# Seven products for eight in an up projection: Strassen's scheme for the ConvFFN of a one-core decoder step

## The chip, the core and the metric

The kernel runs on one core of one Trainium2 chip. TensorE (PE in the profile, with its weight loads as PEld) multiplies; VectorE (DVE), ScalarE (ACT) and GpSimd (POOL) do the elementwise work; SyncE (SP) issues most transfers. Each engine has a queue of its own and takes its instructions in order; semaphores tie the queues together. A matmul writes to PSUM, from which DVE and ACT read; the other operands lie in SBUF.

The metric is the device time of one execution in microseconds.

## The reference

One inference step of a decoder layer, for 512 prompt positions and a sample group of 8 sequences with 4 positions each, together 544 tokens of width 1024. The mixer (input projection, RG-LRU branch, sliding-window attention, gates, output projection, norms) comes first and is all but untouched by the change. What matters is the feed-forward part behind it:

```python
def _conv_ffn(h, prev, w_up, conv_w, conv_b, w_down):
    u = h @ w_up                                             # 1024 -> 8192
    u, conv_state = _causal_dwconv(u, prev, conv_w, conv_b)  # width 3, over positions
    val, gate = jnp.split(u, 2, axis=-1)
    return (jax.nn.gelu(gate, approximate=True) * val) @ w_down, conv_state   # 4096 -> 1024
...
    f, ffn_state = _conv_ffn(_rmsnorm(x, norm_ffn_pre[l]), ffn_prev, w_up[l], ffn_conv_w[l], ffn_conv_b[l], w_down[l])
    x = x + _rmsnorm(f, norm_ffn_post[l])
```

All inputs and outputs are float32. Outputs are y for both groups and the new states, among them the last two rows of u before the convolution.

## The kernel before

**Precision.** A product in float32 is made of three matmuls in a reduced format: each operand is split into a high and a low part, and high x high, high x low and low x high are summed in PSUM. A weight tile is loaded in float32 ("raw", 512 KB), and split in two units of 128x512: ACT writes the high part (`wsplit_hi`, L271), DVE subtracts it from the raw tile for the low part (`wsplit_lo`, L276). Activations are split in the same way.

**Tiling.** Everything is feature-major: 128 features on the partitions, 544 tokens along them. Tokens are taken in two halves of 256 and 288 (`HALF`). One half column tile of a projection is 8 k x 3 = 24 matmuls into one PSUM bank (`mmhalf`, all matmuls at L144), followed by its evacuation (`done`) and a round of side work (`tick`, `sides`).

**Feed-forward.** The 8192 columns of w_up are 64 column tiles: tile p (value) and tile 32 + p (gate) form a pair. Four pairs' first token halves are computed early, while the second half of the tokens is still in its norms (`norm_chain`). `up_a` and `up_b` copy the halves into a tile `u` (ACT, L1121 and L1129; the sample columns by DVE, L1130), move the convolution states (POOL, L1128, L1131, L1132), and convolve in three taps: the first on ACT (L1134), two on DVE (the helper `stt`, L156). `glu` applies GELU (ACT, L1142) and multiplies (DVE, `z`), then splits the result into `fH` and `fL` (ACT L1149; the helper `sub`, L147). The down projection runs in four quarters of the 4096 features: 8 pairs, then 8 column tiles x 2 halves of 24 matmuls each, `pmdn`. Quarter 0 is copied out of PSUM by ACT (L1225), later ones are added to `ft` by DVE (the helper `add`, L153). The last quarter takes the second token half first; its final norm (`finish_b`: statistics `pst_o`, `rep_o`, POOL additions at L1254, transposes `pyo` at L1262) runs under the products of the first half, whose own end is `finish_a` (L1274).

**Order.** PE's order is the program's order throughout. ACT's and DVE's are so in the mixer and left to a planner in the feed-forward part; POOL's and SP's are the planner's. Tiles come from rings of buffers (53 slots "s", 10 temporaries, 5 raw weight tiles, 12 split units, 8 PSUM banks): a step whose ring is full waits for the oldest user to finish. Splits run a fixed number of column tiles ahead of their use (`upto`).

Of the kernel before, what the change touches and what calls it, by code (L numbers as in the profile page):

```python
# [17 lines left out]
P = 128  # L18
# [7 lines left out]
HALF = ((0, 256), (256, NT))  # L26
NH = 8
# [12 lines left out]
S_BUFS = 53  # L40
# [3 lines left out]
SLOT = 576  # L44
LEAD = 2
NORM_TICKS = (2.5, 3.5)
HP = 150
NSTART = (1, 1)
YA = (1, 1)
YB = (1, 1)  # L50
EARLY = 8
# [52 lines left out]
def hawk_step(ctx, tc, I, O):  # L104
# [3 lines left out]
    cp = ctx.enter_context(tc.tile_pool(name="const", bufs=1))  # L108
# [10 lines left out]
    mixer = ExitStack()  # L119
    mixer.enter_context(tc.manual_schedule(engines={act.engine, dve.engine}))  # L120
# [37 lines left out]
    # Side work runs in stages between the half column tiles of the main products. A half tile's results are  # L158
    # taken out of PSUM while the next one runs.
# [32 lines left out]
    ident = cp.tile([P, P], F32, name="ident")  # L192
    make_identity(nc, ident)
    ones = cp.tile([P, P], F32, name="ones")
    pool.memset(ones, 1.0)
    epst = cp.tile([P, 1], F32, name="epst")
    pool.memset(epst, EPS)

# [1 line left out]
    w_in, w_up, w_dn = I["w_in"][0], I["w_up"][0], I["w_down"][0]  # L200

    def wsrc(key):
        kind = key[0]
        if kind in ("wr", "wi"):
            return I["lru_" + kind][0, 4 * key[1]:4 * key[1] + 4].rearrange("n c d -> c n d")
        w = {"in": w_in, "lo": I["w_lru_o"][0], "ao": I["w_attn_o"][0], "out": I["w_out"][0], "up": w_up,
             "dn": w_dn}[kind]
        c = key[-1]
        if kind == "dn":
            w = w[key[1] * D:(key[1] + 1) * D, :]  # L210
        return w[:, c * P:(c + 1) * P].rearrange("(k p) n -> p k n", p=P)
# [9 lines left out]
    ffn_seq = []  # L221
    nxt = 0
    for q in range(4):
        while nxt < min(32, 8 * q + 8 + LEAD):
            ffn_seq.append(("pair", nxt))
            order += [("up", nxt), ("up", 32 + nxt)]
            nxt += 1
        ffn_seq.append(("down", q))
        order += [("dn", q, c) for c in range(8)]
    early_up = [("up", j) for p_ in range(EARLY // 2) for j in (p_, 32 + p_)]  # L230
    wpos = {k: i for i, k in enumerate(order)}
    in_slots = {("out", c) for c in range(3, 8)} | {("dn", 3, c) for c in range(3, 7)} | set(early_up[3:])
    in_slots |= {("in", c) for c in qkv_order[3:FIRST]}
    in_temps = {("dn", 3, 7)}
# [15 lines left out]
    def wclaim(target):  # L250
        """Units (half column tiles) up to the target that are not split yet; loads run two tiles ahead."""
        target = min(target, 2 * len(order))
        for i in range(len(wraw), min(len(order), (target + 1) // 2 + 2)):
            if target:
                wload(i)
        got = list(range(wnext[0], target))
        wnext[0] = max(wnext[0], target)
        return got

    def wsplit_hi(un):  # L260
        i, u = un // 2, un % 2
        hl = []
        for x in "hl":
            if order[i] in in_slots or order[i] in in_temps:
                t_ = (S if order[i] in in_slots else T)(f"w{x}{u}_{wname(i)}", F32R)[:, 0:512]
# [15 lines left out]
    class Full:  # L281
        """Eight operand tiles [P, NT], high and low parts."""

        def __init__(self, name):
            self.name, self.t = name, {}
# [5 lines left out]
        def get(self, k, a, j):  # L291
            lo, hi = HALF[a]
            return self.t[k][j][:, lo:hi]

    class Halves:
        """Eight operand tiles, two to a slot, the token halves apart."""
# [4 lines left out]
        def get(self, k, a, j):  # L301
            n = HALF[a][1] - HALF[a][0]
            if (k // 2, a) not in self.t:
                self.t[k // 2, a] = [S(f"{self.name}{x}{k // 2}_{a}", F32R) for x in "HL"]
            return self.t[k // 2, a][j][:, (k % 2) * n:(k % 2 + 1) * n]

    def mmhalf(ps, key, X, a, ks=range(KD)):
        n = HALF[a][1] - HALF[a][0]
        if key == order[0] and a == 0:
            # the parts in the order in which they get ready  # L310
# [34 lines left out]
    warm = cp.tile([P, 1], F32, name="warm")  # L345
# [26 lines left out]
    pv = cp.tile([P, 96], F32, name="pv")  # L372
    # keeps the tensor engine's clock up until the first tokens are there
# [7 lines left out]
    def newton_rstd(r, v, s_, sq):  # L381
        """r = (sq / D + EPS) ** -0.5 from the hardware's square root and one Newton step."""
# [80 lines left out]
    fv = cp.tile([P, 256], F32, name="fv")  # L463
# [10 lines left out]
    # recurrent states: rows 0..23 conv (b, i), rows 24..31 h0 (b)  # L474
# [7 lines left out]
    def params():  # L482
# [13 lines left out]
        # c = 8 softplus(-lambda) = 8 (max(-lambda, 0) + log1p(exp(-|lambda|)))  # L496
# [39 lines left out]
    def attn_tables():  # L536
# [6 lines left out]
        # one copy of each head's row per query, read back with a row pitch one short: the Toeplitz band  # L543
# [32 lines left out]
    # shifted part of the sample caches goes straight through DRAM  # L576
# [70 lines left out]
    def softmax_a(s3, nh, sink, nm):  # L647
        """s3 [P, nh, n] scores to exponentials in place; sink [P, nh]."""
# [150 lines left out]
    stage = cp.tile([P, KD, 36], F32, name="stage")  # L799
    L = Full("l")  # L800
# [130 lines left out]
    # the first column tiles run on the first token half alone while the second is still being normed  # L931
# [23 lines left out]
    # while softmaxes run, the gates' logits wait for their sigmoids  # L955
# [24 lines left out]
    # x again, feature-major, for the residual  # L980
# [19 lines left out]
    M = Halves("m")  # L1000

    def lo_done(c):
        def f(a, ps):
            lo, hi = HALF[a]
# [16 lines left out]
    def stats(acc, nch, nm, more=None):  # L1021
        """acc [P, 128 nch]: squares summed over feature tiles; returns rstd [P (tokens), nch]."""
# [17 lines left out]
    def spread(dg, n, nm):  # L1040
        """The diagonal of rstd (tokens) to a row replicated over the partitions, in PSUM."""
# [14 lines left out]
    h2 = Halves("h2_")  # L1056
    mt = [S(f"mt{c}") for c in range(8)]

    def norm_chain(a, acc):
        lo, hi = HALF[a]  # L1060
        n = hi - lo
        nch = (n + P - 1) // P
        with tc.high_priority(offset=HP):
            dg = diag(stats(acc, nch, f"m{a}"), n, f"m{a}")
        yield YA[a]
        with tc.high_priority(offset=HP):
            rep = spread(dg, n, f"m{a}")
            acc2 = T(f"accx{a}")
            for c in range(8):
                m_ = mt[c][:, lo:hi]  # L1070
                stt(m_, m_, pv[:, G_POST + c:G_POST + c + 1], rep[:, :n], ALU.mult, ALU.mult)
                pool.tensor_tensor(out=x1[c][:, lo:hi], in0=x1[c][:, lo:hi], in1=m_, op=ALU.add)  # L1072
                sq_sum(acc2, x1[c][:, lo:hi], n, c == 0, f"x{a}_{c}")
        yield NORM_TICKS[a]
        with tc.high_priority(offset=HP):
            dg = diag(stats(acc2, nch, f"f{a}"), n, f"f{a}")
        yield YB[a]
        with tc.high_priority(offset=HP):
            rep = spread(dg, n, f"f{a}")
            for c in range(8):  # L1080
                t_ = T(f"h2t{a}_{c}")
                stt(t_[:, :n], x1[c][:, lo:hi], pv[:, G_FPRE + c:G_FPRE + c + 1], rep[:, :n], ALU.mult, ALU.mult)
                act.activation(h2.get(c, a, 0), t_[:, :n], AF.Copy)
                sub(h2.get(c, a, 1), t_[:, :n], f32(h2.get(c, a, 0)))

    def out_done(c, acc):
        def f(a, ps):
            lo, hi = HALF[a]
# [4 lines left out]

    for a in range(2):
        acc = T(f"acc{a}")
        for c in range(8):
            target = upto(("out", c), 1, 3) if a == 0 else 2 * (wpos["up", 0] + min(c, EARLY))
            step(("out", c), M, a, out_done(c, acc), target=target, quick=True)
        start_at(now[0] + NSTART[a], norm_chain(a, acc))

# [1 line left out]
    # conv states: DRAM rows (b, i) of 8192 seen as (b, i, m) rows of 1024  # L1102
    sfT = cp.tile([P, KD, 16, 8], F32, name="sfT")
    stage_p = cp.tile([P, KD, 2, 8], F32, name="stage_p")
    sf_rows = RAW("sf_rows")
    nc.sync.dma_start(out=sf_rows, in_=I["state_ffn_conv"].rearrange("o b i (m n) -> (o b i m) n", n=D))
    ut = {}
# [10 lines left out]
    def up_a(j, ps):  # L1118
        u = ut[j] = T(f"u{j}")
        pool.memset(u[:, 0:2], 0.0)  # L1120
        act.activation(u[:, 2:258], ps[:, 0:256], AF.Copy)  # L1121

    def up_b(j, ps):
        m, c = j // 8, j % 8
        u = ut[j]
        uv = u[:, SEQ + 2:SEQ + 2 + 6 * DB].rearrange("p (b i) -> p b i", b=DB)
        sv = sfT[:, c, :, m].rearrange("p (b i) -> p b i", b=DB)
        pool.tensor_copy(uv[:, :, 0:2], sv)  # L1128
        act.activation(u[:, 258:514], ps[:, 0:256], AF.Copy)  # L1129
        dve.tensor_copy(uv[:, :, 2:6], ps[:, 256:288].rearrange("p (b t) -> p b t", b=DB))  # L1130
        pool.tensor_copy(sv, uv[:, :, 4:6])  # L1131
        pool.tensor_copy(stage_p[:, c, :, m], u[:, SEQ:SEQ + 2])  # L1132
        y = T(f"uc{j}")
        act.activation(y[:, 0:FLATU], u[:, 0:FLATU], AF.Copy, scale=fv[:, j:j + 1])  # L1134
        for t in (1, 2):
            stt(y[:, 0:FLATU], u[:, t:t + FLATU], fv[:, 64 * t + j:64 * t + j + 1], y[:, 0:FLATU], ALU.mult, ALU.add)
        return y

    F = Full("f")

    def glu(p_, yv, yg):
        act.activation(yg[:, 0:FLATU], yg[:, 0:FLATU], AF.Gelu_apprx_tanh, bias=fv[:, 224 + p_:225 + p_])  # L1142
# [206 lines left out]
```

## Time and profile before

| | |
|---|---|
| time of the runs, median (lowest to highest of 3) | 1052.47 us (1051.9 to 1053.2) |
| span of the profiled execution, first to last instruction | 1048.6 us |
| what lies around the span, against the median of the runs | 3.9 us |
| PE busy | 1036.7 us, 99% |
| DVE, ACT, POOL busy | 614.3, 522.6 and 167.7 us |
| first and last start of an up matmul (`pmup`) | 446.2 and 984.6 us |
| first and last start of a down matmul of the first quarters and the last (`pmdn`) | 573.0 and 1039.5 us |
| moved by DMA | 100.06 MB |

The page records the profiled execution's span and not its device time apart from it; the median of the runs stands beside it. An engine is busy while it has an instruction in work; matmuls are pipelined, so that a busy PE is read with the spacing of its matmuls. In a row of a view that groups instructions stand the line, the engine, the operation, what it writes and reads, its shapes and count, then the busy time, the mean duration in ns, and the idle time of the engine before it with what ended it. A tile's rows show min/median/max in ns, and the first and last start. A row of the chain shows its start, its length and what it was. A row of a stretch (start:end) shows for PE, PEld, DVE, ACT and POOL the busy time and instruction count, then the mean granted clock of TensorE, the DMA engines' busy share and GB/s.

### The profile page before, as it was taken

To read this page: it belongs to the slowest core of one execution; us is meant where nothing else is said; L and a number is where in the kernel's file an instruction comes from. 1 tells how busy PE (TensorE), PEld (TensorE's weight loads), DVE (VectorE), ACT (ScalarE), POOL (GpSimd) and SP (SyncE) were. 2 spreads that over 40 slices of the span, in tenths; PEclk is the share of its full clock that TensorE was granted. 3 is DMA by queue.
4 is the path that set the end of the run, shared out by engine and by line. 5 is a ranking of instruction groups with operands and counts; after the bars stand their busy time and mean duration, and the time that the engine had idled before them with its cause. 6 is when DMAs were issued, how large, how long until landed. Compare 5 with 4: busy or idle time off the path is not lost.

```text
span 1048.6 us, 20365 instructions
## 1 busy us (share of the span) xinstructions
PE 1036.7 (99%) x8183; PEld 1029.0 (98%) x8183; DVE 614.3 (59%) x1242; ACT 522.6 (50%) x1115; POOL 167.7 (16%) x481
## 2 busy tenths in 40 slices
PE   8999999999999999999999999999999999999997
PEld 7999999999999999999999999999999999999997
DVE  5477687537737564877766326665346664366643
ACT  5544545468387445646555335554235552255633
POOL 2231000003105330222311001110001110011111
PEclk8999999999999999999999999999999999999999
DMA  7822222332323354222223322322322322322212
GB/s 238 262 75 80 75 85 83 101 101 82 101 60 103 102 149 143 81 81 81 62 82 93 90 81 84 98 82 86 96 81 83 99 81 86 97 82 83 64 39 86
DMA packets 172839, 100.06 MB, mean 95 GB/s; under 512 B 4482, under 2 KB 168946, under 8 KB 172712
## 3 DMA queue, kind: packets, MB, share of 16 engines
q1 hardware_dynamic: 170152, 91.94, 29.8%
q0 software_dynamic: 2160, 6.30, 1.7%
q8 instruction: 64, 1.05, 0.4%
q10 hardware_dynamic: 432, 0.52, 0.1%
q14 instruction: 31, 0.25, 0.1%
HBM read 95.44 MB, written 6.91 MB: 98 GB/s over the span
## 4 chain that ended last, share of the span: by engine, by line
PE 95%; POOL 1%; DMA 1%; DVE 1%; SPq 1%; ACT 1%; issue 0%; DVEq 0%; POOLq 0%; ACTq 0%
PE pmup L144 36%; PE pmin L144 20%; PE pmdn L144 18%; PE pmlo L144 5%; PE pmao L144 5%; PE pmout L144 4%; PE pg L144 1%; PE psc L144 1%; POOL x L1072 1%; DMA raw_in<-in_w_in_dram 1%; PE pvp L144 1%; SPq L353 1%; PE dn3h L144 1%; PE pt L693 1%; PE pso L144 0%; PE pxx L992 0%
## 5 line engine op out<-in xcount | busy, mean ns | idle before, releaser
L144 PE MATMUL pmup<-h_H,wh_up 128*128 128x288 f32 (+1 forms) x1024 | 296.7, 290 | 0.1
L144 PE MATMUL pmup<-h_H,wl_up 128*128 128x288 f32 (+1 forms) x1024 | 295.9, 289 | 0.0
L144 PE MATMUL pmup<-h_L,wh_up 128*128 128x288 f32 (+1 forms) x1024 | 295.6, 289 | 0.0
L144 PEld LDWEIGHTS pmup<-h_H,wh_up 128*128 128x128 f32 x1024 | 194.0, 189 | 0.4 <-ACT u L1121 0.3
L144 PEld LDWEIGHTS pmup<-h_L,wh_up 128*128 128x128 f32 x1024 | 194.1, 190 | 0.1
L144 PEld LDWEIGHTS pmup<-h_H,wl_up 128*128 128x128 f32 x1024 | 194.2, 190 | 0.0
L144 PE MATMUL pmin<-hH,wh_in 128*128 128x256 f32 (+1 forms) x576 | 167.8, 294 | 0.0
L144 PE MATMUL pmin<-hH,wl_in 128*128 128x256 f32 (+1 forms) x576 | 165.4, 289 | 0.1
L144 PE MATMUL pmin<-hL,wh_in 128*128 128x256 f32 (+1 forms) x576 | 164.9, 288 | 0.0
L144 PE MATMUL pmdn<-fH,wh_dn 128*128 128x256 f32 (+1 forms) x496 | 143.6, 290 | 0.0
L144 PE MATMUL pmdn<-fH,wl_dn 128*128 128x256 f32 (+1 forms) x496 | 143.0, 288 | 0.0
L144 PE MATMUL pmdn<-fL,wh_dn 128*128 128x256 f32 (+1 forms) x496 | 143.0, 288 | 0.0
L276 DVE TENSOR_TENSOR wl_up<-raw_up,wh_up 128x512 fp32r<-128x512 f32 x128 | 88.3, 693 | 80.2 <-ACT wh_up L271 78.6
L156 DVE SCALAR_TENSOR_TENSOR uc<-u,fv,uc 128x560 f32<-128x560 f32 x128 | 103.0, 805 | 52.9 <-ACT uc L1134 50.8
L271 ACT ACTIVATE wh_up<-raw_up 128x512 fp32r<-128x512 f32 x128 | 79.2, 626 | 83.7 <-PE pmup L144 47.9
L144 PEld LDWEIGHTS pmin<-hH,wh_in 128*128 128x128 f32 x576 | 109.6, 192 | 1.6 <-ACT kH L591 0.6
L144 PEld LDWEIGHTS pmin<-hH,wl_in 128*128 128x128 f32 x576 | 109.1, 191 | 0.3 <-DVE wl_in L276 0.3
L144 PEld LDWEIGHTS pmin<-hL,wh_in 128*128 128x128 f32 x576 | 108.8, 190 | 0.0
L1132 POOL COPY stage_p<-u 128x2 f32<-128x2 f32 x64 | 29.5, 462 | 437.7 <-ACT u L1129 437.7
L144 PEld LDWEIGHTS pmdn<-fH,wh_dn 128*128 128x128 f32 x496 | 94.1, 190 | 0.1
L144 PEld LDWEIGHTS pmdn<-fL,wh_dn 128*128 128x128 f32 x496 | 94.1, 190 | 0.1
L144 PEld LDWEIGHTS pmdn<-fH,wl_dn 128*128 128x128 f32 x496 | 94.1, 190 | 0.0
(367 smaller groups left out, 1930.7 us busy)
## 6 DMA issues: line engine op xcount, KB each, us to landing
raw_up<-in_w_up_dram SPq DMA_DIRECT2D x64, 512.0 KB, 4.0
raw_in<-in_w_in_dram SPq DMA_DIRECT2D x36, 512.0 KB, 3.8
raw_dn<-in_w_down_dram SPq DMA_DIRECT2D x32, 512.0 KB, 3.7
raw_ao<-in_w_attn_o_dram SPq DMA_DIRECT2D x8, 512.0 KB, 3.8
raw_lo<-in_w_lru_o_dram SPq DMA_DIRECT2D x8, 512.0 KB, 3.9
raw_out<-in_w_out_dram SPq DMA_DIRECT2D x8, 512.0 KB, 3.8
x<-in_x_prompt_dram SPq DMA_DIRECT2D x8, 256.0 KB, 12.2
xx<-in_x_prompt_dram SPq DMA_DIRECT2D x4, 512.0 KB
```

Source lines behind the costliest of these rows:

```text
L144: pe.matmul(out, l, r, start=start, stop=stop)
L156: dve.scalar_tensor_tensor(out=out, in0=a, scalar=s_, in1=b, op0=op0, op1=op1)
L271: act.activation(hl[0], raw, AF.Copy)
L276: (eng or dve).tensor_tensor(out=hl[1], in0=raw, in1=f32(hl[0]), op=ALU.subtract)
L353: nc.sync.dma_start(out=xt[i, z][:n, 0:512], in_=src[:, 512 * z:512 * z + 512])
L693: pe.transpose(pt[:, (2 * ch + j) * P:(2 * ch + j + 1) * P], s3[:, j, ch * P:(ch + 1) * P], ident)
L1072: pool.tensor_tensor(out=x1[c][:, lo:hi], in0=x1[c][:, lo:hi], in1=m_, op=ALU.add)
L1132: pool.tensor_copy(stage_p[:, c, :, m], u[:, SEQ:SEQ + 2])
```

## The change

The up projection of a pair is seen as a 2x2 block product: the rows of blocks are the tile pair (value tile, gate tile), the inner blocks are the first and last four of the eight k, the columns of blocks are the two token halves, now 272 tokens each (`HALF2`). Instead of the 8 block products it makes 7, in the form of Strassen's scheme with shared sums: operand `b11, b21, b22` are blocks of the normed tokens, `t1` to `t4` sums of them, made once after the second norm chain and kept. Four weight sums `p1` to `p4` are made for each pair on POOL (`sum_`), split like any weight unit, and each product is 4 k x 3 = 12 matmuls of 272 columns. Products that belong together accumulate in one PSUM bank; the others are combined afterwards by ACT copies, DVE additions out of PSUM and POOL subtractions.

In the eight pairs of `EARLY` two products (a11 with b11, a12 with b21) are made ahead, during the second norm chain, and the other five later; their value tile is loaded a second time for that. The down projection runs in eight chunks of four pairs; its half column tiles, now 12 matmuls each, are set between the products of later pairs by a list (`plan`). A product or a down half tile is one slot; results are taken up in the next slot, taps and gating in up to nine further slots (`later`, `slot`). Splits run four units ahead of their use, sums two more, loads eight. ACT's and DVE's order is now the program's order in this part too. The residual x1 is written to DRAM and loaded again near the end, to free its slots.

The core of the diff; the removed code is the old `up_a`, `up_b`, `up_done`, `glu` and the loop over `ffn_seq`:

```diff
+HALF2 = ((0, 272), (272, NT))
+CH = 4
+CHAIN = 10
+AHEAD = 4
+LOADS = 8
+E_BUFS = 5
+P_BUFS = 5
+SUMS = 2
-EARLY = 8
+EARLY = (1, 3, 5, 6, 7, 8, 9, 10)
...
     def norm_chain(a, acc):
...
+            for k in range(2):
+                sub(first(k), first(k), second(k))
+                act.activation(operand2("t1", k, 0), first(k), AF.Copy)
+                yield 0.5
+            for k in range(2):
+                pool.tensor_tensor(out=second(k), in0=second(k), in1=second(2 + k), op=ALU.subtract)
+                sub(operand2("t1", k, 1), first(k), f32(operand2("t1", k, 0)))
+                yield 0.5
+            for k in range(2):
+                add(first(k), first(k), second(2 + k))
+                pool.tensor_tensor(out=first(2 + k), in0=first(2 + k), in1=first(k), op=ALU.subtract)
+            for nm, src in (("t3", second), ("t2", first)):
+                yield 0.5
+                for k in range(2):
+                    split_operand(nm, k, src(k))
+            for nm, src in (("b22", second), ("t4", first)):
+                yield 0.5
+                for k in range(2):
+                    split_operand(nm, k, src(2 + k))
             for c in range(8):
...
+                nc.sync.dma_start(out=x1d[c], in_=x1[c][:, 0:NT])
...
+    XOF = {"a11": "b11", "p1": "t1", "p3": "t3", "p2": "t2", "a12": "b21", "p4": "b22", "a22": "t4"}
+    plan, ready, due = [], {}, 0
+    halves_ = [("dn", q, c, a) for q in range(QL) for c in range(8) for a in range(2)]
+    for p_ in range(32):
+        prods = [("s", p_, nm) for nm in (("p1", "p3", "p2", "a22", "p4") if p_ in EARLY else XOF)]
+        for x in prods:
+            plan.append(x)
+            ready[p_] = len(plan) + CHAIN
+            due += 0 if p_ <= CH else (16 // CH if p_ < 32 - CH + 1 else 2) / len(prods)
+            while due > 0.99 and halves_ and len(plan) >= ready.get(CH * halves_[0][1] + CH - 1, len(plan) + 1):
+                plan.append(halves_.pop(0))
+                due -= 1
+    plan += halves_
...
+    def sum_(p_, nm):
+        r1, r2 = first_raw(p_), raws["up", 32 + p_]
+        a11, a12, a21, a22 = r1[:, 0:4, :], r1[:, 4:8, :], r2[:, 0:4, :], r2[:, 4:8, :]
+        a, b = {"p1": (a21, a22), "p3": (a11, a21), "p2": (psums.get((p_, "p1")), a11),
+                "p4": (psums.get((p_, "p2")), a12)}[nm]
+        psums[p_, nm] = pp.tile([P, 4, P], F32, tag="p", name=f"{nm}_{p_}")
+        pool.tensor_tensor(out=psums[p_, nm], in0=a, in1=b, op=ALU.add)
...
+    def product(ps, ws, nm, start, stop):
+        for k in range(4):
+            wh, wl = (ws[j][:, k, :] for j in range(2))
+            xh, xl = operand(nm, k, 0), operand(nm, k, 1)
+            for i, (w, x) in enumerate(((wh, xh), (wh, xl), (wl, xh))):
+                pe.matmul(ps[:, :HN], w, x, start=start and k == 0 and i == 0, stop=stop and k == 3 and i == 2,
+                          skip_group_check=True)
...
+    def slot(k=1, lag=1):
+        for f in todo.pop(turn[0], []):
+            f()
+        if k:
+            consumed(k, lag)
+        turn[0] += 1
+        round_()
...
+        def v_():
+            keep_("e7")
+            pool.tensor_tensor(out=e["e7"], in0=e["e7"], in1=e["e5"], op=ALU.subtract)
+        def u2_c22():
...
+            u2 = e["e1"]
+            sub(u2, u2, ps["b"][:, :HN])
+            ug = utile(jg)
+            for o, z in zip(halves2(ug, e["e7"]), halves2(ug, u2)):
+                pool.tensor_tensor(out=o[0], in0=o[1], in1=z[1], op=ALU.subtract)
+        def c12():
+            for o, z in zip(halves2(ut[jv], ps["c"]), halves2(ut[jv], e["e1"])):
+                add(o[0], z[1], o[1])
+            states(jv)
+        def c21():
+            sub(ut[jg][:, 2:2 + HN], ps["e"][:, :HN], e["e1"])
+            states(jg)
...
+    for z in range(0, len(EARLY), 2):
+        early_pairs(EARLY[z:z + 2])
+        if z == 2:
+            ffn_prev()
+    for i, x in enumerate(plan):
+        if x[0] == "s":
+            pair(*x[1:])
+            slot()
+        else:
+            _, q, c, a = x
+            down(q, c, a, down_done(q, c))
+            slot(a)
...
     for a in (1, 0):
         acc = T(f"acc3{a}")
...
+        for c in range(8):
+            down(QL, c, a, last_done(c, acc))
+            slot()
+        while todo:
+            slot(0)
         start_at(now[0] + 0.5, finish_b(acc) if a else finish_a(acc))
```

More of the change, by code (lines that the diff above doesn't have):

```diff
@@ L26 @@
 HALF = ((0, 256), (256, NT))
+HALF2 = ((0, 272), (272, NT))
+HN = 272
+BP = SEQ - HN
 NH = 8
@@ L220, in hawk_step @@
     order += [("out", c) for c in range(8)]
[L221 to L230, printed above, removed]
     wpos = {k: i for i, k in enumerate(order)}
-    in_slots = {("out", c) for c in range(3, 8)} | {("dn", 3, c) for c in range(3, 7)} | set(early_up[3:])
-    in_slots |= {("in", c) for c in qkv_order[3:FIRST]}
-    in_temps = {("dn", 3, 7)}
+    in_slots = {("out", c) for c in range(3, 8)} | {("in", c) for c in qkv_order[3:FIRST]}
     wraw, wunits, wnext = {}, {}, [0]
@@ L291, in get @@
         def get(self, k, a, j):
-            lo, hi = HALF[a]
+            lo, hi = self.half[a]
             return self.t[k][j][:, lo:hi]
-    class Halves:
+    class Pairs:
+        half = HALF2
         def __init__(self, name):
@@ new lines, in hawk_step, with load @@
+    plan += halves_
+    units = [("e", EARLY[z + y], u) for z in range(0, len(EARLY), 2) for u in range(2) for y in range(2)]
+    units += [x[:3] for x in plan if x[0] == "s" or x[3] == 0] + [("dn", QL, c) for c in range(8)]
+    raws, usplit, psums, used = {}, {}, {}, [0, 0, 0, 0]
+    def load(key):
+        if key in raws:
+            return
+        raw = rp.tile([P, KD, P], F32, tag="raw", name="raw_" + "_".join(str(z) for z in key))
+        if key[0] == "dn":
+            _, q, c2 = key
+            raw = raw.rearrange("p (k y) n -> p k (y n)", y=2)
+            src = w_dn[q * CH * P:(q + 1) * CH * P, 2 * c2 * P:(2 * c2 + 2) * P]
+        else:
+            j = key[1]
+            src = w_up[:, j * P:(j + 1) * P]
+        raws[key] = raw
+        nc.sync.dma_start(out=raw, in_=src.rearrange("(k p) n -> p k n", p=P))
@@ new lines, in ahead, with upto_, consumed @@
+    def ahead(n, lag=1):
+        def upto_(z, m, f):
+            while used[z] < min(m, len(units)):
+                f(units[used[z]])
+                used[z] += 1
+        upto_(0, n + LOADS, lambda key: [load(r) for r in needs(key)])
+        while used[2] < min(n, len(units)):
+            m = used[2] + 1
+            upto_(1, m + SUMS, do_sum)
+            upto_(2, m, do_high)
+            upto_(3, m - lag, do_low)
+        upto_(3, n - lag, do_low)
+    at = [0]
+    def consumed(k=1, lag=1):
+        at[0] += k
+        ahead(at[0] + AHEAD, lag)
@@ new lines, in hawk_step, with later, early_pairs @@
+    turn, todo = [0], {}
+    def later(k, f, *args):
+        todo.setdefault(turn[0] + k, []).append(lambda: f(*args))
+    def slot(k=1, lag=1):
[5 more added lines that the diff above has]
+        round_()
+    ec = {}
+    def early_pairs(ps_):
+        pss = {}
+        for u in range(2):
+            for p_ in ps_:
+                if u == 0:
+                    pss[p_] = PX(f"pu11_{p_}")
+                    ec[p_] = S(f"ec{p_}")
+                product(pss[p_], usplit["e", p_, u], ("b11", "b21")[u], u == 0, u == 1)
+                later(1, act.copy, ec[p_][:, u * HN:(u + 1) * HN], pss[p_][:, :HN])
+                slot(1, 0)
@@ L1228, in down_done, with x1_again @@
         return f
-    for kind, q in ffn_seq:
-        if kind == "pair" and q >= EARLY // 2:
-            for j in (q, 32 + q):
-                for a in range(2):
-                    step(("up", j), h2, a, up_done(j), quick=True)
-        elif kind == "down" and q < 3:
-            for c in range(8):
-                for a in range(2):
-                    step(("dn", q, c), Quarter(q), a, down_done(q, c), quick=True)
-    start_at(now[0] + 2, ffn_states())
+    x1r = {}
+    def x1_again():
+        for c in range(8):
+            x1r[c] = S(f"x1r{c}")
+            nc.sync.dma_start(out=x1r[c][:, 0:NT], in_=x1d[c])
+        yield 8
+        for i in range(2):
+            for kk in range(2):
+                px = PX(f"px1{i}_{kk}")
+                for j in range(4):
+                    pe.transpose(px[:, j * P:(j + 1) * P], x1r[4 * kk + j][:, i * P:(i + 1) * P], ident)
+                t_ = S(f"xtok{i}_{kk}")
+                act.copy(t_[:, 0:512], px)
+                xtok[i, kk] = t_
+                yield
```

394 lines of the change are left out of this document (251 added, 143 removed).

## The prediction

> **What bounds the kernel now.** I read the engines' busy shares first, then the chain that ended last, then the chain in order of time, then one stretch of the feed-forward part by engine.
>
> ```profile
> span 1048.6 us, 20365 instructions
> ...
> PE 1036.7 (99%) x8183; PEld 1029.0 (98%) x8183; DVE 614.3 (59%) x1242; ACT 522.6 (50%) x1115; POOL 167.7 (16%) x481
> ...
> PE 95%; POOL 1%; DMA 1%; DVE 1%; SPq 1%; ACT 1%; issue 0%; DVEq 0%; POOLq 0%; ACTq 0%
> ...
> 573.18 48.32 PE pmdn L144 x384
> 621.50 97.07 PE pmup L144 x768
> ...
> 621.50:766.88 145.38, 145.38 (x1154) 145.38 (x1154) 78.40 (x135) 62.20 (x114) 13.97 (x64) 1.00 0.30 88
> ```
>
> TensorE (PE) is 95% of the chain. The last row is eight pairs of up tiles with one quarter of the down projection: no idle time on PE, full clock, VectorE (DVE) 78.4 of 145.4 us, ScalarE (ACT) 62.2, GpSimd (POOL) 14.0, DMA 0.30. The two chain rows give the prices: 97.07 / 768 = 0.1264 us for an up matmul, 48.32 / 384 = 0.1258 for a down one. A pair costs 97.07 / 8 + 48.32 / 8 = 18.2 us.
>
> The sum is made against the profiled span of 1048.6 us. The median of the runs shown is 1052.5, 3.9 us above it, and I carry those 3.9 over unchanged. The three runs lie within 1.3 us; 0.2% (2.1 us) is about what can be told from no change.
>
> **Matmuls removed.** A pair had 2 tiles x 8 k x 2 halves x 3 = 96 up matmuls; seven products x 4 k x 3 make 84, all of 272 columns where 256 and 288 alternated. Pairs named in EARLY also come to 84 (two products ahead, five later). So 32 x 12 = 384 go: 384 x 0.1264 = **48.5 us**. The down matmuls stay 1536. A slot of the new plan, 12 matmuls, is 1.52 us, and an ordinary pair with its four down halves is 11 slots, 16.7 us. If PE remains the bound, this is the whole change.
>
> **What is added on the other engines.** These groups give durations:
>
> ```profile
> L276 DVE TENSOR_TENSOR wl_up<-raw_up,wh_up 128x512 fp32r<-128x512 f32 x128 | 88.3, 693 | 80.2 <-ACT wh_up L271 78.6 <-PE pmup L144 1.0
> L271 ACT ACTIVATE wh_up<-raw_up 128x512 fp32r<-128x512 f32 x128 | 79.2, 626 | 83.7 <-PE pmup L144 47.9 <-PE pmdn L144 34.7 <-PE pmout L144 1.0
> L156 DVE SCALAR_TENSOR_TENSOR uc<-u,fv,uc 128x560 f32<-128x560 f32 x128 | 103.0, 805 | 52.9 <-ACT uc L1134 50.8
> L156 DVE SCALAR_TENSOR_TENSOR z<-uc,fv,uc 128x512 f32<-128x512 f32 x32 | 24.1, 752 | 25.4 <-ACT uc L1142 25.4
> L156 DVE SCALAR_TENSOR_TENSOR z<-uc,fv,uc 128x32 f32<-128x32 f32 x32 | 7.9, 246 | 0.0
> L147 DVE TENSOR_TENSOR fL<-z,fH 128x544 fp32r<-128x544 f32 x32 | 23.3, 730 | 4.4 <-ACT fH L1149 1.3
> L153 DVE TENSOR_TENSOR ft<-ft,pmdn 128x256 f32<-128x256 f32 (+1 forms) x46 | 20.1, 436 | 46.9 <-PE pmdn L144 46.8
> ...
> 701.32 0.69 DVE L276 TENSOR_TENSOR wl_up<-raw_up,wh_up 128x512 fp32r<-128x512 f32 x1
> 701.92 0.18 DVE L1130 COPY u<-pmup 128x32 f32<-128x32 f32 x1
> ```
>
> ACT gets three more weight splits a pair: 62.2 / 8 + 3 x 0.63 = 9.7 us of 16.7. It is not the bound.
>
> DVE: the last two rows start 0.60 apart, so a queued instruction costs its duration less 0.09. An ordinary pair then takes nine low parts (seven up, two down) x 0.61, four taps x 0.72 (two directly behind their own input, some 0.1 more each), z 0.83 in its two pieces, fL 0.64: 10.0 us that read two SBUF tensors. It also takes 2.7 us that read PSUM: four ft additions (twice as many, because the down chunks are half as long) and the four combinations of products, priced like ft. Together 12.7 of 16.7 us.
>
> POOL gets four sums of 128x512, e7-e5 and c22 a pair. No sum of that shape is in the trace. These rows bound it and show what happens when it meets DVE:
>
> ```profile
> L1007 POOL TENSOR_TENSOR gl<-gl,ga x16: 732/1146/1190, 344.2 to 395.6; 128x256 f32<-128x256 f32 x8, 128x288 f32<-128x288 f32 x8
> L869 POOL TENSOR_TENSOR xc<-xc,lt x8: 1407/1444/1934, 256.2 to 333.8; 128x568 f32<-128x568 f32 x8
> L276 DVE TENSOR_TENSOR wl_ao<-raw_ao,wh_ao x16: 677/686/1834, 230.5 to 273.7; 128x512 fp32r<-128x512 f32 x16
> ...
> 253.30 1.13 POOL L860 TENSOR_TENSOR lt<-rg 128x568 f32<-128x568 f32 x1
> 253.46 1.51 DVE L276 TENSOR_TENSOR wl_ao<-raw_ao,wh_ao 128x512 fp32r<-128x512 f32 x1
> ...
> 344.00 0.69 DVE L276 TENSOR_TENSOR wl_lo<-raw_lo,wh_lo 128x512 fp32r<-128x512 f32 x1
> 344.17 1.11 POOL L1007 TENSOR_TENSOR gl<-gl,ga 128x256 f32<-128x256 f32 x1 [4.17 <-DVE gl L150]
> 386.54 0.73 POOL L1007 TENSOR_TENSOR gl<-gl,ga 128x256 f32<-128x256 f32 x1 [1.89 <-DVE gl L150]
> ...
> 424.94 1.65 DVE L156 SCALAR_TENSOR_TENSOR mt<-mt,pv,rep_m 128x256 f32<-128x256 f32 x4
> 425.59 3.00 POOL L1072 TENSOR_TENSOR x<-x,mt 128x256 f32<-128x256 f32 x4 [28.67 <-DVE mt L156]
> ```
>
> Alone, the POOL add takes 0.73 us at 256 columns (386.54) and 1.41 at 568 (the least of L869), so by the line between them 1.29 at 512, an estimate; 0.77 at 272 and 0.70 at 240.
>
> At 253.30 POOL is first: DVE's low part beside it takes 1.51 instead of 0.69 and ends 0.54 after POOL does. At 344.00 DVE is first: the POOL add takes 1.11 instead of 0.73 and ends 0.59 after DVE does, which is its own time less 0.14. The last two rows are the exception: DVE reads `rep_m` from PSUM, and four POOL adds run in 0.75 each beside it. So a POOL op and a DVE op with two SBUF inputs take turns. Put between two low parts, a POOL op of duration S costs DVE S - 0.14 + 0.54 - 0.60 = S - 0.20: 1.09 for a sum, 0.57 for e7-e5, 0.50 for c22, nothing for the 0.2 us copies. A pair costs 4 x 1.09 + 1.07 = 5.4 us of DVE time, unless DVE is idle or reading PSUM meanwhile.
>
> An ordinary pair then needs 10.0 + 5.4 = 15.4 us if POOL hides all of DVE's 2.7 us on PSUM, and 18.1 if it hides none, against 16.7 on PE. So DVE, at half use in the old kernel, becomes the engine to watch.
>
> **Stage by stage**, counting DVE's and POOL's instructions in the new program's own order (both ends: all of DVE's PSUM reading hidden, none):
> - 16 early products and pairs 0 to 4, 47 slots without down halves, 71.3 us of PE. DVE: 42 low parts, 16 taps, the second norm chain and the splitting of t1 to t4 and b22, 55.7 us on two SBUF inputs and 15 on PSUM and small ones; POOL: 24 sums and 17 other big adds, 38.9. That is 94.5 to 109.7. PE is fed about 5 us ahead (four units), so it waits 18 to 33.
> - pairs 5 to 10, 55 slots, 83.4 us: 54.9 + 34.4 to 99.7; waits of 6 to 16.
> - pairs 11 to 28, 18 x 16.7 = 300: 282 to 330; 0 to 30.
> - pairs 29 to 31, 41 us: 44 to 49; 3 to 8.
>
> The waits sum to 27 to 87 us. I take four fifths hidden, 21 + 8 + 0 + 4 = **33 us**: the row at 425.59 shows that a POOL op passes a PSUM-reading one freely, and when DVE is the late engine, POOL's sums stand waiting for the low parts to free one of five buffers, so one is nearly always ready. The product combinations on DVE (u2 = e1 - P2 and its like) also wait for PE. Queued behind each are low parts for products three slots on, and PE waits for those; that is the same 4.5 us of lead, counted above.
>
> ```profile
> raw_up<-in_w_up_dram SPq DMA_DIRECT2D x64, 512.0 KB, 4.0
> ```
>
> On POOL the next pair's sums stand ahead of e7-e5. Their weights land in 4.0 us and are issued over five slots ahead, so I cost this, the second load of eight tiles (4 MB at a DMA share of 0.30) and the eight x1 writes in SP's queue at nothing. If that cover goes, the price is one 4 us load each time.
>
> **The end.**
>
> ```profile
> L144 PE MATMUL pst_o<-ones,acc x10: 168/250/250, 1013.6 to 1039.9; 128*128 128x1 f32 x10
> L1262 PE MATMUL pyo<-ident,ft x24: 270/272/273, 1027.0 to 1035.2; 128*128 128x128 f32 x16, 128*32 128x128 f32 x8
> ```
>
> The second token half's final norm takes 1013.6 to 1027.0, 13.4 us, before it is transposed, under 24 us of products of the first half. Now that cover is 8 slots, 12 us, and PE meets these transposes ahead of the first half's statistics: 1.5 to 2 us late, and two of three tiles go out last. +3 us (0 to 6).
>
> Sum: 1052.5 - 48.5 + 33 + 3 = **1040 us**.
>
> **Rivals.**
> 1. *PE stays the bound*: the turn-taking costs little because lead absorbs it. For: DVE alone needs 12.7 of 16.7. Against: in the first 47 slots DVE's 71 us of own work already equals PE's 71, and then every POOL op shows. With 5 us of waits: 1052.5 - 48.5 + 3 + 5 = 1012, down to 1008.
> 2. *Slower: turns cost more.* Place: DVE's queue, from the first early product on; price: every us of PSUM reading that no POOL op covers. With two fifths hidden the waits are 27 + 12 + 11 + 6 = 56 and the time 1063; with none, 87 and 1094. It decides below about half hidden, where the waits exceed 45.5 us. For: L276's 1834 ns. The Trainium skill, page "SBUF — State Buffer", section "Who interferes with whom", says that whoever issues first has the shared port pair for the whole instruction and the other is fully blocked. By that rule, a sum costs all of its 1.29 us, a pair 6.6, and the sum comes to some 1070. The trace agrees in kind, but 0.2 us of each op overlapped.
> 3. *Waits in one piece slow the clock.*
>
> ```profile
> 0.00:20.00 20.00, 15.83 (x89) 15.63 (x90) 11.70 (x33) 11.55 (x26) 6.44 (x20) 0.83 0.85 267
> L440 PE MATMUL ps_ta<-ident,x x16: 421/421/477, 11.2 to 14.5; 128*128 128x128 f32 x16
> ```
>
> The mean granted clock of the first 20 us is 0.83, which is 6.8 us at half speed if it falls to half, and a transpose there takes 421 ns against 272 (L1262). If the 21 us of the first stage came as six waits of over 3 us, each followed by 6.8 us at half speed, that adds 6 x 3.4 = 20: 1060. Against: 47 slots can share 21 us at 0.45 each. The Trainium skill, page "TensorE: Matmul & The Clock Gate", section "HAM oscillation — how this bites in real kernels", puts the limit at idle gaps of about 3.4 us.
>
> **Chances.** My forecast's case, 1022 to 1050: 0.40. PE-bound: 0.15. Turns dearer: 0.30. Clock: 0.08. A balance within 2.1 us of before: 0.07. So faster 0.55, same 0.07, slower 0.38. The range 1008 to 1066 reaches rival 1's end and the nearer half of rival 2; the forecast's own range is 1022 to 1050.
>
> **What would show it.** Right: 4224 up and down matmuls at 0.126 us; idle time on PE before products of pairs 0 to 4, ended by DVE's low parts; DVE over 85% there; low parts and sums lengthened when they overlap; little idle time from pair 11 on. Wrong: PE above 98% through pairs 0 to 10 (rival 1), idle time on PE in pairs 11 to 28 ended by DVE (rival 2), a granted clock under 1 after 446 us (rival 3), or waits ended by ACT or DMA.

## The result and the profile after

The changed kernel takes **1063.28 us** (median of 4 runs, 1060.7 to 1064.75), against 1052.7 for the kernel before: 1.0103 times its time, 95% interval 1.0086 to 1.012. It is slower by 1%, where the prediction said 1040. The profiled execution is the fastest of the four: a span of 1058.6 us, 10.0 more than before.

The page's summary of the changed kernel (span, busy times, VectorE by slices, chain that ended last):

```profile
span 1058.6 us, 20166 instructions
...
PE 1007.2 (95%) x7803; PEld 987.1 (93%) x7803; DVE 859.6 (81%) x1474; ACT 566.0 (53%) x1217; POOL 486.0 (46%) x701
...
DVE  5477687537737464789999999999999999999965
...
PE 47%; DVE 42%; issue 7%; DMA 1%; ACT 1%; SPq 1%; POOL 0%; POOLq 0%; DVEq 0%; ACTq 0%
```

PE carried 95% of the chain before; now VectorE (DVE) carries 42% of it, and from the nineteenth slice to the thirty-eighth it is busy for 90% of the time or more. The stretches of the prediction, in order (length, then busy time of PE, its weight loads, DVE, ACT and POOL, then the granted clock): the 16 early products, pairs 0 to 4, pairs 5 to 10, pairs 11 to 28, pairs 29 to 31.

```profile
448.00:483.60 35.60, 30.37 (x218) 29.33 (x217) 29.45 (x63) 19.73 (x47) 14.57 (x16) 0.90 0.56 167
483.60:553.90 70.30, 56.30 (x374) 52.69 (x373) 70.30 (x84) 38.38 (x74) 58.15 (x67) 0.90 0.25 70
553.90:648.00 94.10, 86.67 (x662) 84.87 (x661) 93.92 (x124) 50.74 (x103) 73.70 (x95) 0.98 0.38 106
648.00:957.80 309.80, 303.40 (x2378) 299.23 (x2377) 309.16 (x436) 162.96 (x308) 212.07 (x273) 1.00 0.33 93
957.80:1003.70 45.90, 41.99 (x326) 40.82 (x325) 44.60 (x64) 26.07 (x49) 27.40 (x42) 1.00 0.30 94
```

DVE is busy for 309.16 / 18 = 17.2 us of a pair of 309.8 / 18 = 17.2 in the fourth stretch. What its instructions now take, and the POOL sums (the third row is those with `p` as an input):

```profile
L167 DVE SCALAR_TENSOR_TENSOR uc<-u,fv,uc 128x560 f32<-128x560 f32 x128 | 172.1, 1345 | 0.8
L158 DVE TENSOR_TENSOR wl_s_p<-p,wh_s_p 128x512 fp32r<-128x512 f32 x128 | 117.0, 916 | 1.5 <-ACT wh_s_p L1270 1.5
L1243 POOL TENSOR_TENSOR p<-p,raw_up 128x512 f32<-128x512 f32 x48 | 81.7, 1701 | 3.2 <-DVE wl_s_p L158 1.6
```

The taps take 1345 ns where they took 805, the low parts of the sums 916, where a low part took 693. One place in order of time shows the turns (start, duration, engine, operation):

```profile
700.42 1.53 POOL L1243 TENSOR_TENSOR p<-raw_up 128x512 f32<-128x512 f32 x1 [2.88 <-DMA raw_up<-in_w_up_dram]
700.72 1.83 DVE L167 SCALAR_TENSOR_TENSOR uc<-u,fv,uc 128x560 f32<-128x560 f32 x1
701.90 1.80 POOL L1243 TENSOR_TENSOR p<-raw_up,raw_up 128x512 f32<-128x512 f32 x1
702.48 1.78 DVE L158 TENSOR_TENSOR wl_s_p<-p,wh_s_p 128x512 fp32r<-128x512 f32 x1
703.66 3.48 POOL L1243 TENSOR_TENSOR p<-p,raw_up 128x512 f32<-128x512 f32 x2
704.18 3.57 DVE L167 SCALAR_TENSOR_TENSOR uc<-u,fv,uc 128x560 f32<-128x560 f32 x2
707.67 0.41 DVE L164 TENSOR_TENSOR ft<-ft,pmdn 128x256 f32<-128x256 f32 x1
```

The raw tile lands, and POOL does the four sums of the next pair in one go. Each DVE instruction beside them waits for one. From 700.72 to 707.67 DVE gets through three taps and one low part, 6.95 us for what takes 3 x 0.72 + 0.61 = 2.8: 1.04 us lost for each sum. The addition that reads PSUM comes only when the four are over.

### The profile page after: what moved, and what is told of

It reads as the page before. It is cut to its first block, busy times and chain, and to the rows that moved or that the text cites. A ratio compares the mean times of both kernels' runs of the same rounds, so it can differ in the third digit from the quotient of the medians.

```text
span 1058.6 us, 20166 instructions
## 1 busy us (share of the span) xinstructions
PE 1007.2 (95%) x7803; PEld 987.1 (93%) x7803; DVE 859.6 (81%) x1474; ACT 566.0 (53%) x1217; POOL 486.0 (46%) x701
## 4 chain that ended last, share of the span: by engine, by line
PE 47%; DVE 42%; issue 7%; DMA 1%; ACT 1%; SPq 1%; POOL 0%; POOLq 0%; DVEq 0%; ACTq 0%
PE pmin L155 20%; DVE uc L167 15%; DVE wl_s_p L158 7%; PE pmlo L155 5%; PE pmao L155 5%; PE pmdn L155 4%; DVE wl_s_a L158 4%; PE pmout L155 4%; DVE z L167 3%; DVE wl_dn L158 3%; DVE ft L164 3%; DVE fL L158 2%; PE pg L155 1%; DVE u L164 1%; DMA raw_in<-in_w_in_dram 1%
## 5 line engine op out<-in xcount | busy, mean ns | idle before, releaser
L167 DVE SCALAR_TENSOR_TENSOR uc<-u,fv,uc 128x560 f32<-128x560 f32 x128 | 172.1, 1345 | 0.8
L158 DVE TENSOR_TENSOR wl_s_p<-p,wh_s_p 128x512 fp32r<-128x512 f32 x128 | 117.0, 916 | 1.5 <-ACT wh_s_p L1270 1.5
L1243 POOL TENSOR_TENSOR p<-raw_up 128x512 f32<-128x512 f32 x32 | 49.4, 1542 | 94.6 <-DMA raw_up<-in_w_up_dram 81.9
L1243 POOL TENSOR_TENSOR p<-p,raw_up 128x512 f32<-128x512 f32 x48 | 81.7, 1701 | 3.2 <-DVE wl_s_p L158 1.6
L1371 ACT ACTIVATE uc<-uc,fv 128x560 f32<-128x560 f32 x32 | 24.4, 762 | 106.6 <-DVE uc L167 106.6
L1270 ACT ACTIVATE wh_s_p<-p 128x512 fp32r<-128x512 f32 x128 | 79.3, 626 | 0.0
L158 DVE TENSOR_TENSOR wl_s_a<-raw_up,wh_s_a 128x512 fp32r<-128x512 f32 x80 | 69.2, 867 | 1.5 <-ACT wh_s_a L1270 1.5
L1360 ACT ACTIVATE uc<-u,fv 128x560 f32<-128x560 f32 x64 | 48.8, 762 | 31.6 <-DVE u L164 27.6
L857 POOL TENSOR_TENSOR lt<-rg 128x568 f32<-128x568 f32 x8 | 10.2, 1275 | 108.1 <-ACT rg L855 108.1
L267 ACT ACTIVATE wh_in<-raw_in 128x512 fp32r<-128x512 f32 x72 | 44.3, 630 | 22.8 <-PE pmin L155 9.8
```

What stands on the lines that cost most here:

```text
L158: dve.tensor_tensor(out=out, in0=a, in1=b, op=ALU.subtract)
L167: dve.scalar_tensor_tensor(out=out, in0=a, scalar=s_, in1=b, op0=op0, op1=op1)
L267: act.activation(hl[0], raw, AF.Copy)
L857: pool.tensor_tensor(out=a2, in0=r, in1=r, op=ALU.mult)
L1243: pool.tensor_tensor(out=psums[p_, nm], in0=a, in1=b, op=ALU.add)
L1270: act.activation(hl[0], src, AF.Copy)
```

## The experiments

**Whose turns.** The sums were left out, then moved to DVE, then the other big POOL additions too.

```diff
# e1: do_sum does nothing; p1, p2, p3, p4 split a22, a21, a11, a12 as they are
# e2 (in sum_)
-        pool.tensor_tensor(out=psums[p_, nm], in0=a, in1=b, op=ALU.add)
+        dve.tensor_tensor(out=psums[p_, nm], in0=a, in1=b, op=ALU.add)
# e3: e2, and in v_ and u2_c22
-            pool.tensor_tensor(..., op=ALU.subtract)
+            dve.tensor_tensor(..., op=ALU.subtract)
```

> Leaves out the four weight sums of a pair: products p1 to p4 take a plain quarter of the weights instead. Matmuls, splits, combinations, taps and loads stay. Theory A (GpSimd's sums take turns with VectorE, and VectorE is the late engine): each sum takes up to 1.09 us from VectorE, so a pair's VectorE time falls from the 17.2 us seen in pairs 11 to 28 to 13.8 or less, under TensorE's 16.7; waits after 448 us fall from 58.6 us to about 15, the time to about 1020, and VectorE is below 90% busy from pair 11 on. Theory B (VectorE's own low parts, combinations and down additions stand in an order that stalls, GpSimd has little to do with it): 1055 to 1065 as now. Theory C (raw weight buffers and loads are late): 1055 to 1065, with waits ended by DMA.

> The four weight sums of a pair move from GpSimd to VectorE, nothing else. Theory A (turn-taking): VectorE does a sum in 0.61 us of its queue where a GpSimd sum costs it up to 1.09; an ordinary pair needs 12.7 + 2.4 + 1.07 = 16.2 us of VectorE, under 16.7; of the 58.6 us of waits about 33 stay, nearly all before pair 5 (VectorE 85 us or more against 71), and the time is about 1037. Theory B (VectorE's own queue is the load, whoever does the sums): 128 x 0.61 = 78 us more on the engine that is already 99.8% busy, 1110 to 1140. Theory C (late loads now block VectorE's queue too): above 1063.

> The four weight sums, e7 - e5 and the two pieces of c22 move from GpSimd to VectorE. Theory A: against the sums alone a pair trades up to 1.07 us of turns for 0.7 us of own work, so some 4 to 8 us less than with the sums alone, about 1031, waits left almost only before pair 5. Theory B: 1120 to 1160, as VectorE gets 96 further instructions of about 0.25 us.

Measured: e1 1016.25 us (0.965 of before, 0.9632 to 0.9668), e2 1032.30 (0.9803, 0.9786 to 0.9821), e3 1031.29 (0.9799, 0.978 to 0.9817). Pairs 11 to 28 in e1, e2 and e3, one row from each kernel's answer by stretch:

```profile
621.30:919.50 298.20, 298.20 (x2377) 298.20 (x2377) 240.81 (x433) 166.06 (x306) 57.39 (x200) 1.00 0.33 96
```

```profile
634.60:933.50 298.90, 298.79 (x2378) 298.34 (x2377) 288.54 (x512) 166.90 (x308) 71.37 (x202) 1.00 0.34 96
```

```profile
633.70:932.70 299.00, 298.87 (x2378) 298.40 (x2377) 285.98 (x566) 166.86 (x308) 55.71 (x150) 1.00 0.34 96
```

PE is busy all but all the time in each of the three, and a pair takes 16.6 us. So in these pairs the waits were neither the order of DVE's own work nor the loads. Three rows give the price of a sum in DVE time: on POOL (309.16 - 240.81) / 72 = 0.95 us, on DVE itself (288.54 - 240.81) / 72 = 0.66. The sums on POOL cost DVE more than doing them. e2 comes out 5 us below theory A's 1037. The step from e2 to e3 was put at 4 to 8 us and is 1.0, within what these runs can tell (each over 2 us wide): e3's 1031 is met, its step is a miss.

**Do the sums cost in a kernel where DVE has slack?** The kernel before, with a sum of each up half tile that nobody reads; then the same for pairs 8 to 31 alone.

```diff
# e4, in wsplit_hi of the kernel before
         act.activation(hl[0], raw, AF.Copy)
+        if order[i][0] == "up":                       # e10: and order[i][1] % 32 >= 8
+            t_ = pp.tile([P, 4, P], F32, ...)
+            pool.tensor_tensor(out=t_, in0=raw, in1=wraw[i][:, 4 - 4 * u:8 - 4 * u, :], op=ALU.add)
```

> The kernel before, with a GpSimd sum of 128x512 added for each half tile of up weights (128 sums, as many as the change has), whose results nobody reads. Theory A (a sum takes about 0.95 us from VectorE, and that shows only where VectorE is the late engine): in the eight pairs from 621 us on VectorE goes from 78.4 to about 109 of 145 us, its low parts from 693 ns to over 850, and the time stays within 3 us of 1053, because TensorE still bounds. Theory B (a GpSimd sum costs time wherever it stands, by SBUF traffic or by delaying buffers): 20 us or more above 1053.

Measured: 1081.02 us (1.0259, 1.0235 to 1.0282), a miss for theory A: the time lies where theory B had it. The DVE figure missed too. The eight pairs of the old stretch:

```profile
645.40:793.90 148.50, 146.67 (x1155) 145.56 (x1153) 92.13 (x135) 60.62 (x113) 62.88 (x96) 1.00 0.30 86
```

DVE goes from 78.4 to 92.1, not to 109: 0.43 us a sum, since 17 of the sums' 47 us now lie in DVE's idle time (in pairs 11 to 28 of the changed kernel it is 0.6 of 119). PE loses 3 us there. Most of the loss is earlier: matmul by matmul the run is 24.0 us behind the kernel before by 548 us (2.5 of it by 240 us, before there is any sum) and 30.2 at the end. The chain in order of time, from that place:

```profile
458.51 4.62 DMA raw_up<-in_w_up_dram
...
463.26 1.28 POOL sum_up L275
...
468.04 1.29 POOL sum_up L275
469.34 1.53 POOL x L1076 x2
470.87 1.47 POOL sum_up L275
472.34 1.72 POOL x L1076 x2
```

The additions to x of the norm chain, for which PE waits, stand in POOL's queue behind sums that wait for their loads. e10 tests that.

> The kernel before with the unread GpSimd sums for pairs 8 to 31 alone (96 sums). In the fourth run 24 of the 28 us that the sums cost fell before 525 us, where the second half's norm chain has GpSimd additions to x, and sums that wait for their loads stand ahead of them. Theory A (a sum costs TensorE nothing while VectorE has slack; it was the place in GpSimd's queue that cost): the FFN's first stretch is as before, the three waits of about 2 us from 660 us on stay, 1053 to 1060. Theory B (each sum costs time wherever it stands): three quarters of the 28 us, about 1074.

Measured: 1057.92 us (1.0052, 1.0036 to 1.0068), in theory A's range. The first product comes 2.8 us later than in the kernel before (2.5 of it by 30 us, so not from the sums), and the distance stays at 2.8 up to 648 us; then it grows to 8.7 in a few waits. On PE itself a small copy of `u` on DVE ends 2.7 us of them:

```profile
PE pmup L145 <- DVE u L1134: 2.7, 5, 0.8
```

So three quarters of the sums cost about a fifth of the 28 us: with slack on DVE a sum costs almost nothing, and the place in POOL's queue was most of the price of e4.

**The threshold, and what PSUM reading hides.**

```diff
# e6, in sum_
-        pool.tensor_tensor(out=psums[p_, nm], ...)
+        (dve if nm in ("p1", "p3") else pool).tensor_tensor(out=psums[p_, nm], ...)
# e7, in down_done, q > 0, sums on POOL
-                add(ft[c][:, lo:hi], ft[c][:, lo:hi], ps[:, :hi - lo])
+                act.activation(ft[c][:, lo:hi], ps[:, :hi - lo], AF.Copy)
```

> Of a pair's four weight sums p1 and p3 go to VectorE, p2 and p4 stay on GpSimd; the rest as in the changed kernel. Theory A with a threshold: 13.4 + 2 x 0.95 + 2 x 0.66 = 16.6 us of VectorE a pair against 16.6 of TensorE, so the waits from pair 11 on nearly go and those before pair 5 fall by half of what moving all of them gave: 1039 to 1043. If each sum moved simply gives a quarter of the 31 us that moving all gave: 1047 to 1049.

> The sums stay on GpSimd; leaves out the additions of a down chunk's result to ft (a ScalarE copy of the chunk takes their place), the twice as many additions that the eight chunks bring. Theory A with the PSUM-reading additions mostly not hidden beside a sum: VectorE has up to 1.4 us less a pair, 15.8 to 16.3 against 16.6, the waits from pair 11 on go: 1046 to 1051. If they were hidden beside the sums, as the prediction took for four fifths of them: 1059 to 1063.

Measured: e6 1050.12 us (0.9965, 0.9948 to 0.9982), e7 1050.66 (0.9985, 0.9971 to 0.9999). Pairs 11 to 28 of e6, then of e7:

```profile
648.20:951.40 303.20, 302.34 (x2378) 298.98 (x2377) 302.56 (x472) 158.88 (x308) 137.38 (x238) 1.00 0.33 95
```

```profile
649.70:950.40 300.70, 299.36 (x2378) 298.49 (x2377) 296.08 (x367) 187.33 (x381) 232.42 (x273) 1.00 0.34 95
```

e6 misses its threshold: DVE needs 302.56 / 18 = 16.8 us a pair, not 16.6. The two sums left on POOL cost (16.8 - 13.4 - 2 x 0.66) / 2 = 1.05 us each, all but the full price, and waits of 4 us stay. The time lies outside both ranges. (Its first product also starts 4.8 us later than the changed kernel's, at 452.8; from the first product to the last down matmul it gains 12.8 us, 585.4 against 598.2, where e2 gains 30.8: less than half, so no threshold helped.) e7 falls in the range for "mostly not hidden". Leaving out four additions, 4 x (0.43 - 0.09) = 1.4 us of DVE's queue, gives (309.16 - 296.08) / 18 = 0.73 a pair. So about half of that PSUM reading had cost nothing, not four fifths, and not because of the sums. Counted in the timeline of the changed kernel, the `ft` additions of pairs 11 to 28 take 25.4 us; 0.7 of them lie beside a sum, 6.9 beside e7 - e5 or c22, as here, and 5.6 beside POOL's small copies:

```profile
711.12 1.69 POOL L1444 TENSOR_TENSOR u<-e,e 128x240 f32<-128x240 f32 x2 [0.42 <-DVE e L158]
711.50 0.44 DVE L164 TENSOR_TENSOR ft<-ft,pmdn 128x288 f32<-128x288 f32 x1
```

**What is left before pair 5.** In e3 the 16 early products take 35.4 us and pairs 0 to 4 take 64.0. PE waits 4.2 us there for ScalarE's copies `ec`. e5 issues the high parts of t1 later; e8 and e9 compute pairs 0, 2 and 4, or 0 and 2, in the plain way.

```diff
# e5: e3, and in norm_chain
             for k in range(2):
                 sub(first(k), first(k), second(k))
-                act.activation(operand2("t1", k, 0), first(k), AF.Copy)
                 yield 0.5
             for k in range(2):
+                act.activation(operand2("t1", k, 0), first(k), AF.Copy)
# e8 (e9: CONV = (0, 2)): e3; b12 is split too, b12 and b22 ahead of t1; and in the plan
+        if p_ in CONV:                                 # CONV = (0, 2, 4)
+            prods = [("s", p_, f"c{u}{a}") for u, a in CSLOTS]
...
+        product(ps, usplit["s", p_, f"c{u}0"], (("b11", "b12"), ("b21", "b22"))[u % 2][a], u % 2 == 0, u % 2 == 1)
```

> All adds on VectorE, as in the third run, and the high parts of t1 are issued to ScalarE half a round later, after both differences. Theory A (the 4 us that TensorE waits for ScalarE's copies ec before 484 us come from ScalarE's queue, where the copies stand behind t1H, which waits for VectorE): most of these 4 us go, 1026 to 1029. Rival (VectorE is the late engine there already, and the later t1H delays the low parts): 1030 to 1034.

> All adds on VectorE, and pairs 0, 2 and 4 are computed in the plain way: eight products of a quarter of the weights with b11, b12, b21, b22, so 12 matmuls more a pair, four low parts instead of seven, no sums and no combinations; b12 is split in addition. Theory A (before pair 5, where no down halves stand between the products, VectorE has more work than TensorE): a plain pair takes 6.5 us less of VectorE and 1.5 us more of TensorE; VectorE's 97 us up to pair 4 become about 80, TensorE's 76 become 81, and the time falls by 10 to 14 us against all adds on VectorE: 1015 to 1020. Rival (what is late there is the chain of norms and operand splits, not VectorE's sum of work): 1028 to 1035, as three pairs cost 4.6 us more of TensorE.

> The same with pairs 0 and 2 alone. Theory A: VectorE about 86 us up to pair 4, TensorE 79: 1019 to 1024, between all adds on VectorE and three plain pairs. Rival: 1028 to 1034.

Measured: e5 1029.72 us (0.977, 0.9744 to 0.9797), e8 **1015.30** (0.9648, 0.9627 to 0.9669), e9 1019.22 (0.9684, 0.9668 to 0.97). The early products and pairs 0 to 4 of e5, then of e8:

```profile
447.00:475.90 28.90, 28.07 (x219) 27.25 (x218) 25.76 (x61) 19.18 (x46) 3.11 (x4) 1.00 0.70 206
475.90:544.60 68.70, 54.45 (x373) 49.94 (x373) 68.53 (x123) 39.51 (x76) 28.57 (x40) 0.93 0.24 70
```

```profile
449.40:483.40 34.00, 30.33 (x218) 28.97 (x217) 30.04 (x67) 19.48 (x46) 5.69 (x9) 0.93 0.64 190
483.40:535.70 52.30, 52.30 (x410) 52.14 (x410) 51.43 (x91) 35.64 (x68) 23.20 (x37) 0.98 0.32 91
```

In e5 the wait for `ec` goes and the first part shrinks by 6.5 us (4.2 are the wait; the clock there is 1.00, where e3 has 0.90), but pairs 0 to 4 grow by 4.7, with DVE busy in 68.5 of 68.7 us: the rival's reason, in the main. The time lies between the two ranges, and 1.6 us from e3 is within the spread of e5's runs. Giving PE three more slots and DVE less work takes 11.7 us off these pairs against e3, PE is then busy throughout, and e8 and e9 both come out as theory A had it. Both also split b12 and b22 ahead of t1, and what that order alone gives was not separated; the third plain pair, with the order the same, is worth 3.9 us. e8 beats the kernel before by 3.5% and the changed one by 4.5% (1015.30 / 1063.28).

## Why the prediction was wrong

- *Matmuls removed, 48.5 us*: right. PE has the time only where it is fed: 198 slots take 298.2 us in e1, 1.51 each.
- *POOL and DVE take turns, S - 0.20 a sum*: right in kind and size. 1.09 was forecast, 1.04 is seen in the row of four, 1.05 in e6; the sum alone was put at 1.29, and one takes 1.28 in e4's chain. As a mean over pairs 11 to 28 it is 0.95. The rule cited from the Trainium skill, page "SBUF — State Buffer", section "Who interferes with whom", by which the first to issue shuts the other out for the whole instruction, would make it all of 1.29; the trace stays below that, as the prediction had it.
- *Four fifths hidden beside PSUM reading*: this step failed. In pairs 11 to 28 DVE's instructions that read PSUM take 45.4 us, 2.5 a pair. Counted in the timeline, 0.7 of the 45.4 lay beside a sum, 6.9 beside e7 - e5 or c22 and 8.9 beside small copies, which the prediction had at nothing: a third beside POOL work of any kind, and next to none beside the sums. The measured 17.2 us a pair fits that: it is 0.9 below the 18.1 with none hidden, but 4 x (1.09 - 0.95) = 0.6 of the 0.9 is the lower mean price of the sums and not hiding. The prediction gave two reasons. The row at 425.59 was thin ground: DVE's four instructions there end at 426.59, beside the first third of POOL's 3.00 us. The other was that late sums stand waiting for low parts to free a buffer, so that one is always ready. The waits of the changed kernel from 440 us on say what POOL waited for instead and, in the second view, what SyncE waited for, which issues the loads (total, times, longest):

```profile
POOL p L1243 <- DMA raw_up<-in_w_up_dram: 81.9, 25, 8.9
...
POOL p L1243 <- DVE wl_s_p L158: 3.5, 4, 1.2
```

```profile
SPq L1225 <- DVE wl_s_a L158: 310.7, 49, 15.5
```

  81.9 us for raw weights, 3.5 for a low part that frees a sum's buffer. The low parts do hold the sums up, but by the raw tiles: a load waits until a low part has read the old tile. Just before the place shown above, one such low part ends at 695.53, the load behind it is issued at 695.55, and the first sum starts at 700.42. The prediction had put these loads at nothing, as issued over five slots ahead. So the sums of a pair come in a row when their load lands, beside whatever DVE then has.
- *Waits of 33 us*: too low. From the first product to the last down matmul it takes 598.2 us (448.0 to 1046.2) against 593.5 before, so 53.2 were added to the 48.5 saved. By stretch, above 1.51 us a slot: 35 in the first 47 slots (2.6 of it other PE work; 21 were taken), 11 in pairs 5 to 10 (8), 11 in pairs 11 to 28 (0), 5 in pairs 29 to 31 (4), 59 of waits in all. Each of the four is inside its bounds. Some 6 us to the good stand against them: 2.4 us of transposes `pyo`, which no longer lie between the products, and for the most part of the rest that a slot takes 1.51 us and not 1.52, over 352 slots. Rival 2, with two fifths hidden, had 27 + 12 + 11 + 6 = 56 us and 1063: it is what happened, in its place and near its waits, and it had 0.30; less than two fifths was hidden, but a sum cost less too. That its 1063 is met to the microsecond is luck: the 3 us more of waits, the 6 us to the good and a first product 1.9 us later all but cancel.
- *First stretch*: it is not all the sums' turns. e1 has no sums and still takes 34.2 us for the 16 early products, which have 24 us of matmuls; with its pairs 0 to 4 (53.5 us) 14 us of waits are left in the 47 slots, of the 32 in the changed kernel. The prediction named no wait for ACT there, and in the changed kernel PE waits 4.8 us for `ec`, which in ACT's queue stands behind t1H.
- *The end, +3 us*: right. From the last down matmul to the end it takes 9.0 us before (1039.6 to 1048.6) and 12.4 after. The first product comes 1.9 us later, which the sum did not have. So 1.9 + 53.2 - 48.5 + 3.4 = 10.0, the difference of the spans.
- *Rival 3, the clock*: it did fall, to half for 6.8 us in each of the two waits of over 4 us (at 476.2 and 489.9), and to half for 3.4 us at 520.6, 547.9 and 568.4, behind waits of only 1.9, 1.9 and 2.7 us, less than the limit that the prediction gives. Among the early products that cost some 2.3 us: in e5, at a clock of 1.00, PE is busy 28.07 us there, against 30.37. In pairs 0 to 4 DVE is busy in 70.30 of 70.30 us, so there a slower PE cost nothing of its own.

## What to carry to other kernels

An operation moved to a second engine isn't free if both read SBUF through turns: count what it takes from the other engine, and compare that with doing it there (0.95 against 0.66 us here). What is "hidden beside" other work needs a row that shows when the hidden work starts: here a load started it, all at once, and the load itself had waited for a buffer. And where a change makes a new engine late in one stretch only, undo the change in that stretch, as the plain pairs do.

## What the runs showed of the hardware

The weight sums on DVE in e3, and one kind of small POOL copy in the changed kernel:

```profile
L1243 DVE TENSOR_TENSOR p<-raw_up 128x512 f32<-128x512 f32 x32 | 21.9, 683 | 0.4 <-DMA raw_up<-in_w_up_dram 0.4
```

```profile
L1352 POOL COPY u<-sfT 128x16 f32<-128x16 f32 x64 | 29.7, 490 | 0.0
```

- A 128x512 addition of two SBUF inputs takes 0.68 us on DVE (e3) and 1.28 on POOL where DVE is idle or reads PSUM (e4's chain); in the changed kernel the POOL one takes 1.70 beside DVE and makes DVE 0.95 later. That falls to 0.43 where DVE, the sums' price included, is busy for 62% of the time (e4).
- Small POOL copies feel it too: the one above took 212 ns in the kernel before. And POOL's queue is in order, so sums that waited for loads, ahead of the norm chain's additions, put PE over 20 us behind (e4).
- The first product starts between 447.0 us (e5) and 452.8 (e6) in kernels that share nearly all the code up to there, so spans of single runs are compared from there on.
